# A hybrid streaming layer on one core: the order of its input projections

## The chip, the cores and the metric

One core of a Trainium2 chip runs the whole layer. The metric is the device time of one execution in microseconds, as the median of several runs. Engines are called TensorE (PE in the rows; PEld is its weight load), VectorE (DVE), ScalarE (ACT), POOL (GpSimd) and SP, which issues most DMAs.

## What is computed

One step of a streaming encoder for 1024 prompt frames and 32 sample frames, 1056 rows in all, model width 1024:

```python
xn = rms_norm(x, norm_mix)
zq, zk, zv, ziq, zik, ziw, zs = _split(xn @ w_in, (512, 256, 256, 512, 64, 8, 1696))
q  = rope_partial(rms_norm(zq, q_gain), pos)          # 8 heads of 64
k  = rope_partial(rms_norm(zk, k_gain), pos)          # 4 heads of 64
qi = rope_partial(ziq, pos); ki = rope_partial(layer_norm(zik), pos)   # indexer
score = sum_h relu(qi_h . ki / 8) * ziw_h / sqrt(8)   # over the keys a chunk may see
keep the top min(256, L // 4) keys of each query      # 256 for the prompt, 136 for the sample
o_att  = softmax(q . k / 8 over the kept keys) @ v
o_rwkv = rwkv7_time_mix(zs)       # token shift, decay, delta rule, group norm, gate; 8 heads
h = x + concat(o_att, o_rwkv) @ w_out
y = h + square(relu(rms_norm(h) @ w_ff1)) @ w_ff2     # hidden width 4096
```

Outputs are y, the keys, the values, the indexer keys, the RWKV state and the last row of zs.

## The kernel before

Every product in 32-bit numbers is made of three in a shorter format: both factors are split into a high and a low part (hi, lo), and high by high, high by low and low by high are added in PSUM. The normalised input stands transposed in SBUF as xh and xl for the whole of the projections. The weights are split where they are needed, in `wprep`: a DMA into `wraw` (three buffers), a ScalarE cast into `wh`, a POOL subtraction into `wl`. There are eight buffers of each in the set x and eight in the set y, exactly one weight group each.

Python code issues work in a chosen order, generators step several strands in turn, and a planner with a timeline of its own then fixes each engine's queue before the run; an engine takes its queue strictly in order. `high_priority(n)` moves instructions n ranks ahead in the planner's list. Memory is a stack of pools: a tile of a pool that was opened where another pool was closed waits for the readers of the tiles that lay there.

The order of the projections before:

- `main`: rows are normalised and transposed (`x_tile`), the indexer's keys and the values are projected (`key_tile`), then the indexer's queries, whose scores go to the tile G (`idx_tile`).
- `main2`: keys (9 tiles of 256 columns, W in set x), then queries (9 tiles of 512 columns, W in set y). Both use `norm_tile`: `proj_tok` (24 matmuls, 16 in the tile of the sample), a copy to the tile zq (three buffers), squares, sums, a power on POOL (`rsqrt_small`, L125), a VectorE multiply (L420), a gain multiply on POOL (L421), four rotation instructions on POOL (L221 to L224) and a DMA out. Queries go to `qd` in DRAM.
- `main3`: the RWKV inputs zs in 14 blocks (`zs_block`, list `ZB`; index 0 is the 64 columns of decay and learning rate, 1 the 96 of the gate, the others 128 columns of r, k or v). A block is 3 times 24 matmuls of 352 columns (L440), two ScalarE passes that empty each bank with the token shift (L449, L450), an addition on POOL (L452) and a DMA to `zsd` in DRAM. They run in seven groups; the third set z was opened for one of them in place of y.

The top-k of the indexer is two chains (`topk`): one with counts on VectorE (L342) for the row tiles 2, 3, 4 and 8, and one with sign passes on ScalarE (L362) for 5, 6 and 7. Each takes 32 steps, a bit of the threshold in each, and then makes the masks (L382 to L404). `step(n)` issues up to n steps of both chains after a tile or block.

The RWKV work is five units of up to 256 tokens. `rwkv_front` prepares a unit: step 1 loads k and makes norms and the decay's small products, step 2 sums the decay (L647), step 3 makes kk, exponentials, and the products k and tha (L669, L671), step 4 makes KB (L681) and the bonus; then come AR and the products G of its four chunks (L712, L715), and a triangular inverse on POOL (`lane_inverse`, L824 to L835). `rwkv_back` carries the state. Three rounds of unit 0's front are issued beside the last blocks (`EARLYF`). Step 4 needs the pool `rb`, which opens after the projections' pools are closed; attention's pool `at` follows it. Unit 1's KB and G are the top-k's tiles KB and G. Attention (`attn_all`, L1064 to L1146) and RWKV are then issued in turn; the output projection and the MLP (L1256, L1320, L1340) come last.

Of the kernel before, what the change touches and what calls it, by code (L numbers as in the profile page):

```python
# [55 lines left out]
BF16 = mybir.dt.bfloat16  # L56
I32 = mybir.dt.int32
AF = mybir.ActivationFunctionType
ALU = mybir.AluOpType
# [4 lines left out]
BIG = 3.0e38  # L64

T = 1056
NT = 9
# [7 lines left out]
def rows_of(t):  # L75
    return 128 if t < 8 else 32
# [74 lines left out]
def phase_a(S, pwx, pwy, pa, pi, px, xp, ps, late):  # L151
    nc, I, O = S.nc, S.I, S.O
# [7 lines left out]
    def wprep(tag, o, n, dve=True):  # L160

        W = []
        pool, size = {"x": (pwx, 328), "y": (pwy, 512), "z": (late.get("pz"), 128)}[tag]
        for k in range(8):
            raw = pwx.tile([128, 512], F32, name="wraw", bufs=3)
            c = 0
            for a, m in runs(o if isinstance(o, list) else [(o, n)]):
                nc.sync.dma_start(raw[:, c:c + m], w_in[k * 128:(k + 1) * 128, a:a + m])
                c += m
            hi = pool.tile([128, size], F32R, name="wh" + tag, bufs=8)  # L170
            lo = pool.tile([128, size], F32R, name="wl" + tag, bufs=8)
            (nc.vector.tensor_copy if dve and k % HIM < HID else nc.scalar.copy)(hi[:, :n], raw[:, :n])
            nc.gpsimd.tensor_tensor(lo[:, :n], raw[:, :n], hi[:, :n].bitcast(F32), op=ALU.subtract)
            W.append((hi, lo))
        return W

# [53 lines left out]
    for t in range(4, NT):  # L230
        n = 664 if t == 8 else 128 * (t + 1)
# [175 lines left out]
    def norm_tile(t, W, H, gain, dst):  # L407

        r = rows_of(t)
        n = H * 64  # L410
        z = pa.tile([128, 512], F32, name="zq", bufs=ZQB)[:r, :n]
        proj_tok(z, t, W, n)
        qk = z.rearrange("p (h d) -> p h d", h=H)
        sq = pa.tile([128, 8, 64], F32, name="sq", bufs=1)[:r, :H]
        nc.scalar.square(sq, qk)
        st = pa.tile([128, 2, 8], F32, name="stq", bufs=2)[:r, :, :H]
        nc.vector.tensor_reduce(st[:, 0], sq, AX.X, ALU.add)
        nc.vector.tensor_scalar(st[:, 0], st[:, 0], 1.0 / 64, 1e-6, op0=ALU.mult, op1=ALU.add)
        rsqrt_small(S, st[:, 1], st[:, 0], H)
        nc.vector.tensor_tensor(qk, qk, st[:, 1][:, :, None].to_broadcast([r, H, 64]), op=ALU.mult)  # L420
        nc.gpsimd.tensor_tensor(qk, qk, gains[:r, gain][:, None, :].to_broadcast([r, H, 64]), op=ALU.mult)  # L421
        rope(qk, t, H)
        nc.sync.dma_start(dst, z)
# [33 lines left out]
    def main():  # L457
        pend = [x_load(0)]
        nc.sync.dma_start(gbc, I["norms"][0:1].partition_broadcast(128))
        nc.sync.dma_start(S.ident, I["ident"])  # L460
        pend.append(x_load(1))
        nc.vector.memset(S.sc[8][:, 544:664], FMAX)
        for X in TK:
            nc.gpsimd.memset(X.cnt, 0.0)
            nc.gpsimd.memset(X.cns, 0.0)
            for j, t in enumerate(X.SL):
                n = S.sc[t].shape[1]
                for i in range(2):
                    nc.gpsimd.memset(X.off[:, i, j:j + 1], float(n - 256 - 256 * i))
        Wa = wprep("x", [(1536, 72), (768, 256)], 328, False)  # L470
        nc.sync.dma_start(cs, I["rope"][0])
        nc.sync.dma_start(sn, I["rope"][1])
        nc.sync.dma_start(gains, I["gains"].partition_broadcast(128))
        nc.sync.dma_start(S.pv, I["pvec"])
        for t in range(NT):
            if t + 2 < NT:
                pend.append(x_load(t + 2))
            x_tile(t, pend[t])
            if t >= LAG:
                key_tile(t - LAG, Wa)  # L480
            if t >= LAG + LAGT:
                key_turn(t - LAG - LAGT)
            if t == WBT:
                Wb = wprep("y", 1024, 512, False)
            if t == CKT:
                cache_keys()
            yield
        for t in range(NT - LAG, NT + LAGT):
            if t < NT:
                key_tile(t, Wa)  # L490
            key_turn(t - LAGT)
        late["W"] = wprep("x", 512, 256)
        for i, t in enumerate(IDXO):
            idx_tile(t, Wb)
            if i >= EI:
                for _ in range(EARLY):
                    next(tk[0], None)
            yield
# [3 lines left out]
    def step(n):  # L502
        for i, g in enumerate(tk):
            m = min(n, left[i])
            left[i] -= m
            for _ in range(m):
                next(g)

    mu1 = pwx.tile([128, 14], F32, name="mu1")

    def main2():
        nc.gpsimd.memset(S.shl, 0.0)
        nc.gpsimd.tensor_scalar(mu1, S.pv[:, 16:30], -1.0, 1.0, op0=ALU.mult, op1=ALU.add)
        W = late["W"]
        Wn = wprep("y", 0, 512)
        for t in range(NT):
            norm_tile(t, W, 4, 1, O["k_prompt"][t * 128:t * 128 + rows_of(t)] if t < 8 else O["k_sample"])
            step(STEP)
        late["W"] = wprep("x", *cols(0))
        for t in range(NT):  # L520
            norm_tile(t, Wn, 8, 0, S.qd[t * 128:t * 128 + rows_of(t)])
            if t == 8:
                S.mb[7] = S.mp.tile([128, 1024], BF16, name="mb7")
            step(STEP)


    gs = [("x", [0]), ("y", [2, 5, 8, 11]), ("x", [3, 6]), ("y", [9, 12]), ("x", [4, 7]), ("z", [10]), ("x", [13, 1])]

    def cols(j):
        o = [(1608 + ZB[i][0], ZB[i][1]) for i in gs[j][1]]  # L530
        return o, sum(n for _, n in o)

    def main3(pool, j0, j1):

        for j in range(j0, j1):
            W = late["W"]
            if j + 1 < len(gs):
                late["W"] = wprep(gs[j + 1][0], *cols(j + 1))
            c = 0
            for i in gs[j][1]:  # L540
                zs_block(i, W, c, pool, mu1)
                c += ZB[i][1]
                step(STEP)
                yield
        if j1 == len(gs):
            for t in range(2):
                n = 128 * (t + 1)
                nc.gpsimd.memset(S.mb[t], 0.0)
                nc.gpsimd.memset(S.mb[t][0:64, n - 64:n], -BIG)
            step(100)  # L550
            yield

    def masks():
        for g in tk:
# [803 lines left out]


STEP = 1  # L1360
PREI = 0
F0 = 200
F1 = 0
# [10 lines left out]
PTB = 2  # L1374
PRE = 2
EARLYF = 3
MA = 8
ATT0 = 0
BOFF = 300
# [5 lines left out]
RORD = (0, 1, 2, 3, 4)  # L1385
# [25 lines left out]
def body(tc, I, O, dbg=None):  # L1411
# [4 lines left out]
    with pool(name="const") as cp, pool(name="dram", space=DRAM) as dp:  # L1416
# [6 lines left out]
        def opened(name, side="left"):  # L1423
            p = pool(name=name, side=side)
            return p, p.__enter__()

        def close(*ps):
            for p in ps:
                p.__exit__(None, None, None)
# [5 lines left out]
        with pool(name="xnt") as xp, pool(name="psA", space=PSUM) as ps:  # L1435
            late = {}
            a_x, pwx = opened("pwx")
            a_y, pwy = opened("pwy")
            a_1, pa = opened("pa")
            with pool(name="pi", side="right") as pi:  # L1440
                with pool(name="px", side="right") as px:
                    m1, m2, m3, masks = phase_a(S, pwx, pwy, pa, pi, px, xp, ps, late)
                    g = m1()
                    for _ in range(NT):
                        next(g)
                with pool(name="pj", side="right") as late["pj"]:
                    for _ in g:
                        pass
            p1b, te = opened("p1b", "right")
            eq = te.tile([128, 2, 1024], F32, name="KB")  # L1450
            S.eq = [eq[:, i] for i in range(2)]
            with pool(name="pq", side="right") as pq:
                m2()
                close(a_1)
                for _ in m3(pq, 0, 4):
                    pass
            close(a_y)
            a_z, late["pz"] = opened("pz")
            rs, S.rs = opened("rs", "right")
            rf, S.rf = opened("rf", "right")  # L1460
            S.ps, S.pr = ps, ("pd", 6 - ACB)
            S.fronts = 0
            with pool(name="pq") as pq:
                g = m3(pq, 4, 7)
                next(g)
                rwkv_setup(S)
                S.kv = {(0, False): attn_load(S, 0, False)}
                gr = rwkv_all(S, RORD)
                for _ in range(EARLYF):
                    next(gr)  # L1470
                for _ in g:
                    pass
            close(a_z, a_x)
        rb, rp = opened("rb")
        at, S.at = opened("at")
        rf2, S.rf2 = opened("rf2", "right")
# [61 lines left out]
```

## Time and profile before

| what | us |
|---|---|
| median of 3 runs | 1797.38 (1795.8 to 1797.55) |
| the profiled execution | 1798.12 |
| its span, first to last instruction | 1796.3 |
| busy: TensorE / VectorE / ScalarE / POOL | 1663.9 / 936.1 / 707.6 / 618.6 |

The span is the time from the program's first instruction to its last; what lies around it is 1.8 us. A matmul is shown with its passage through the array, so that TensorE reads as busy when matmuls overlap; the spacing of their starts is what a stream of them costs. Instructions on POOL are rough. The granted clock of TensorE is 1.00 at 2.4 GHz and 0.50 at 1.2 GHz, and a stretch with both shows a mean.

### The profile page before, as it was taken

The numbers are of one execution on the slowest core, as the hardware profiler recorded it, in microseconds if no ns is written. First come the engines' busy times: TensorE is split into PE (matmuls) and PEld (weight loads), VectorE is DVE, ScalarE is ACT, GpSimd is POOL, SyncE is SP. The second block draws the span as 40 slices with busy tenths as digits, with TensorE's granted clock in tenths as the row PEclk, the third lists the DMA queues.
The fourth block names the chain that finished last, engine by engine and source line by source line (L and its number), as shares of the span: only waits on it lengthen the run. The fifth ranks groups of instructions, "written<-read, shape, count | busy, mean of one in ns | idle before, by whom it ended". The sixth has DMA issues, their size and how long they took to land.

```text
span 1796.3 us, 30013 instructions
## 1 busy us (share of the span) xinstructions
PE 1663.9 (93%) x11686; PEld 1509.2 (84%) x11686; DVE 936.1 (52%) x1996; ACT 707.6 (39%) x1549; POOL 618.6 (34%) x919
## 2 busy tenths in 40 slices
PE   7999979986569898999899999999999999999999
PEld 6787779986456777767678799999999999999998
DVE  6477889975878687577562533222222222222224
ACT  6365667897446344344641331222222121212120
POOL 7468863353543443056210021222222222222120
PEclk9999989996559697798899999999999999999999
DMA  7211131323110202140323341111111111111105
GB/s 218 54 36 43 42 88 64 110 68 92 29 27 14 40 24 57 26 101 17 98 76 123 121 125 49 46 48 45 49 37 53 42 53 42 47 44 51 36 16 172
DMA packets 180775, 113.25 MB, mean 63 GB/s; under 512 B 51969, under 2 KB 169817, under 8 KB 180633
## 3 DMA queue, kind: packets, MB, share of 16 engines
q1 hardware_dynamic: 171800, 107.00, 21.4%
q10 hardware_dynamic: 8832, 4.33, 0.9%
q8 instruction: 92, 1.51, 0.4%
q14 instruction: 51, 0.41, 0.1%
HBM read 86.29 MB, written 25.01 MB: 62 GB/s over the span
## 4 chain that ended last, share of the span: by engine, by line
PE 63%; DVE 12%; ACT 5%; POOL 4%; issue 3%; DMA 2%; SPq 0%; DVEq 0%; ACTq 0%; POOLq 0%
PE pd L1320 20%; PE pr L1340 10%; PE pc L1340 5%; PE po L1340 5%; PE pd L1256 3%; PE po L1139 2%; DVE AR L342 2%; ACT AR L362 2%; PE ptr L1123 2%; PE pr L1256 2%; PE acc L440 2%; DVE L L824 1%; PE pr L712 1%; POOL tl L829 1%; POOL Yl L831 1%
## 5 line engine op out<-in xcount | busy, mean ns | idle before, releaser
L1320 PE MATMUL pd<-hh,w1h 128*128 128x352 f32 x768 | 248.6, 324 | 2.2 <-issue 1.4
L1320 PE MATMUL pd<-hh,w1l 128*128 128x352 f32 x768 | 248.2, 323 | 0.7 <-DVE w1l L1187 0.7
L1320 PE MATMUL pd<-hl,w1h 128*128 128x352 f32 x768 | 247.5, 322 | 0.0
L1326 DVE TENSOR_TENSOR h2l<-rl,h2h 128x352 fp32r<-128x352 f32 x96 | 56.9, 592 | 277.3 <-ACT h2h L1325 277.3
L1324 POOL TENSOR_TENSOR rl<-rl 128x352 f32<-128x352 f32 x96 | 85.2, 888 | 215.5 <-ACT rl L1323 215.5
L1186 ACT CAST w2h<-w2r 128x512 fp32r<-128x512 f32 x64 | 39.7, 621 | 293.0 <-PE po L1340 144.8
L1320 PEld LDWEIGHTS pd<-hh,w1h 128*128 128x128 f32 x768 | 144.7, 188 | 2.8 <-issue 1.7
L1320 PEld LDWEIGHTS pd<-hh,w1l 128*128 128x128 f32 x768 | 144.8, 189 | 0.9 <-DVE w1l L1187 0.9
L1320 PEld LDWEIGHTS pd<-hl,w1h 128*128 128x128 f32 x768 | 145.3, 189 | 0.0
L1187 POOL TENSOR_TENSOR w2l<-w2r,w2h 128x512 fp32r<-128x512 f32 x32 | 41.6, 1299 | 299.3 <-ACT w2h L1186 288.8
L1340 PE MATMUL pr<-h2h,w2l 128*128 128x352 f32 x384 | 124.3, 324 | 0.0
L1340 PE MATMUL pr<-h2h,w2h 128*128 128x352 f32 x384 | 124.3, 324 | 0.0
L1340 PE MATMUL pr<-h2l,w2h 128*128 128x352 f32 x384 | 124.1, 323 | 0.0
L362 ACT ACTIVATE AR<-G,cnd 128x768 bf16<-128x768 f32 (+2 forms) x93 | 96.7, 1040 | 42.2 <-DVE cnd L367 36.8
L1323 ACT ACTIVATE rl<-pd 128x352 f32<-128x352 f32 x96 | 44.3, 463 | 143.4 <-PE pd L1320 136.9
L1346 DVE TENSOR_TENSOR ya<-ya,pr 128x352 f32<-128x352 f32 x84 | 43.8, 521 | 101.0 <-PE pr L1340 101.0
L829 POOL TENSOR_TENSOR tl<-L,Yl 128x56 f32<-128x56 f32 (+22 forms) x155 | 65.9, 425 | 60.5 <-DVE L L824 50.0
L1105 ACT ACTIVATE s<-s,m 32x544 f32<-32x544 f32 (+8 forms) x72 | 55.4, 770 | 74.8 <-DVE m L1102 74.6
L1123 PE MATMUL ptr<-ident,s 128*128 128x128 f32 (+2 forms) x328 | 69.4, 321 | 16.2 <-ACT s L1105 11.2
L1325 ACT CAST h2h<-rl 128x352 fp32r<-128x352 f32 x96 | 46.6, 485 | 75.3 <-POOL rl L1324 75.3
L1340 PEld LDWEIGHTS pr<-h2l,w2h 128*128 128x128 f32 x384 | 72.3, 188 | 0.1
L1340 PEld LDWEIGHTS pr<-h2h,w2h 128*128 128x128 f32 x384 | 72.2, 188 | 0.1
(443 smaller groups left out, 4655.1 us busy)
## 6 DMA issues: line engine op xcount, KB each, us to landing
w1r<-in_w_ff_dram SPq DMA_DIRECT2D x32, 512.0 KB, 4.1
w2r<-in_w_ff_dram SPq DMA_DIRECT2D x64, 256.0 KB, 2.9
zsd<-zm SPq DMA_DIRECT2D x12, 528.0 KB, 2.7
wraw<-in_w_in_dram SPq DMA_DIRECT2D x24, 256.0 KB, 2.7
wraw<-in_w_in_dram SPq DMA_DIRECT2D x40, 128.0 KB, 2.2
x<-in_x_prompt_dram SPq DMA_DIRECT2D x8, 512.0 KB, 5.0
hres<-hd ACTq DMA_DIRECT2D x16, 256.0 KB, 3.3
out_dram<-hres SPq DMA_DIRECT2D x16, 256.0 KB, 2.3
```

The costliest lines, as they stand in the source:

```text
L362: nc.scalar.activation(junk2[:r, :n], S.sc[t][:r, :n], AF.Sign, bias=c_of(j, r), scale=-1.0, accum_out=cnt[:r, j:j + 1])
L829: eng.tensor_tensor(t_, L[:, 0:j, j:j + 1].to_broadcast([128, j, w]), Y[:, j:j + 1, m:16].to_broadcast([128, j, w]), op=ALU.mult)
L1105: nc.scalar.activation(s, s, AF.Exp, bias=m[:, i:i + 1], scale=-1.0, accum_out=w.m[:, 6 + h:7 + h])
L1123: nc.tensor.transpose(p[:x, i, h, :r], w.s[h][:, c0 + i * 128:c0 + i * 128 + x], S.ident[:r, :r])
L1256: nc.tensor.matmul(acc[:r], a[:, k], b, start=(i == 0), stop=(i == 23))
L1320: nc.tensor.matmul(acc, a[:, k], m[:, k, o:o + n], start=(i == 0), stop=(i == 23))
L1323: nc.scalar.activation(rl, acc, AF.Relu)
L1324: nc.gpsimd.tensor_tensor(rl, rl, rl, op=ALU.mult)
L1325: nc.scalar.copy(h2h[:, o:o + n], rl)
L1326: nc.vector.tensor_tensor(h2l[:, o:o + n], rl, h2h[:, o:o + n].bitcast(F32), op=ALU.subtract)
L1340: nc.tensor.matmul(acc, a[:, k], m[:, o:o + n], start=(i == 0), stop=(i == 11))
L1346: nc.vector.tensor_tensor(y, y, acc, op=ALU.add)
```

## The change

The RWKV inputs come directly behind the indexer, in five groups that take the sets x and y in turn. Then set y is closed, the RWKV pools are opened, and the keys and the queries come last, the queries in two passes of 256 columns, all three with weights in set x. The three early rounds of unit 0's front are issued beside them, three tiles after each round (`KQ`), the rest of the tiles after that. A block issues two steps of the top-k (`ZSTEP`) in place of one, a tile one. The first load of attention's keys and values, and the masks of the first two row tiles, come after the last query tile. The pool `pa`, with the tiles of `norm_tile`, is opened below `pwy` and stays until the end of the projections.

```diff
-        pool, size = {"x": (pwx, 328), "y": (pwy, 512), "z": (late.get("pz"), 128)}[tag]
+        pool, size = {"x": (pwx, 328), "y": (pwy, 512)}[tag]
...
-        late["W"] = wprep("x", 512, 256)
+        late["W"] = wprep("x", *cols(0))
...
     def main2():
-        nc.gpsimd.memset(S.shl, 0.0)
-        nc.gpsimd.tensor_scalar(mu1, S.pv[:, 16:30], -1.0, 1.0, op0=ALU.mult, op1=ALU.add)
-        W = late["W"]
-        Wn = wprep("y", 0, 512)
-        for t in range(NT):
-            norm_tile(t, W, 4, 1, O["k_prompt"][t * 128:t * 128 + rows_of(t)] if t < 8 else O["k_sample"])
-            step(STEP)
-        late["W"] = wprep("x", *cols(0))
-        for t in range(NT):
-            norm_tile(t, Wn, 8, 0, S.qd[t * 128:t * 128 + rows_of(t)])
-            if t == 8:
-                S.mb[7] = S.mp.tile([128, 1024], BF16, name="mb7")
-            step(STEP)
-    gs = [("x", [0]), ("y", [2, 5, 8, 11]), ("x", [3, 6]), ("y", [9, 12]), ("x", [4, 7]), ("z", [10]), ("x", [13, 1])]
+        for c in (512, 0, 256):
+            W = late["W"]
+            if c < 256 or c == 512:
+                late["W"] = wprep("x", 0 if c == 512 else 256, 256)
+            for t in range(NT):
+                r = rows_of(t)
+                dst = S.qd[t * 128:t * 128 + r, c:c + 256] if c < 512 else O["k_prompt"][t * 128:t * 128 + r] if t < 8 else O["k_sample"]
+                norm_tile(t, W, 4, int(c == 512), dst)
+                step(STEP)
+                yield
+        S.mb[7] = S.mp.tile([128, 1024], BF16, name="mb7")
+        for t in range(2):
+            n = 128 * (t + 1)
+            nc.gpsimd.memset(S.mb[t], 0.0)
+            nc.gpsimd.memset(S.mb[t][0:64, n - 64:n], -BIG)
+        step(100)
+        yield
+    gs = [("x", [0, 3, 6]), ("y", [9, 12, 2, 5]), ("x", [8, 11]), ("y", [4, 7, 10, 13]), ("x", [1])]
...
-    def main3(pool, j0, j1):
-        for j in range(j0, j1):
+    def main3(pool):
+        nc.gpsimd.memset(S.shl, 0.0)
+        nc.gpsimd.tensor_scalar(mu1, S.pv[:, 16:30], -1.0, 1.0, op0=ALU.mult, op1=ALU.add)
+        for j in range(len(gs)):
             W = late["W"]
-            if j + 1 < len(gs):
-                late["W"] = wprep(gs[j + 1][0], *cols(j + 1))
+            late["W"] = wprep(gs[j + 1][0], *cols(j + 1)) if j + 1 < len(gs) else wprep("x", 512, 256)
             c = 0
             for i in gs[j][1]:
                 zs_block(i, W, c, pool, mu1)
                 c += ZB[i][1]
-                step(STEP)
-                yield
+                step(ZSTEP)
...
+ZSTEP = 2
+KQ = 3
...
             a_x, pwx = opened("pwx")
+            a_1, pa = opened("pa")
             a_y, pwy = opened("pwy")
-            a_1, pa = opened("pa")
...
             with pool(name="pq", side="right") as pq:
-                m2()
-                close(a_1)
-                for _ in m3(pq, 0, 4):
-                    pass
+                m3(pq)
             close(a_y)
-            a_z, late["pz"] = opened("pz")
...
-            with pool(name="pq") as pq:
-                g = m3(pq, 4, 7)
-                next(g)
-                rwkv_setup(S)
-                S.kv = {(0, False): attn_load(S, 0, False)}
-                gr = rwkv_all(S, RORD)
-                for _ in range(EARLYF):
-                    next(gr)
-                for _ in g:
-                    pass
-            close(a_z, a_x)
+            g = m2()
+            next(g)
+            rwkv_setup(S)
+            gr = rwkv_all(S, RORD)
+            for i in range(EARLYF):
+                next(gr)
+                for _ in range(KQ):
+                    next(g, None)
+            for _ in g:
+                pass
+            S.kv = {(0, False): attn_load(S, 0, False)}
+            close(a_1, a_x)
```

## Rows read from the trace of the kernel before

**Rows 1.** Windows by stage: stretch, length, busy us (instructions) by engine PE/PEld/DVE/ACT/POOL, clock, DMA.

```profile
114.00:219.00 105.00, 102.02 (x571) 85.34 (x569) 78.44 (x142) 60.34 (x140) 86.49 (x110) 1.00 0.15 44
219.00:252.00 33.00, 21.16 (x120) 18.25 (x120) 32.33 (x66) 20.63 (x42) 25.81 (x30) 0.90 0.33 85
252.00:416.00 164.00, 152.67 (x920) 149.64 (x920) 132.70 (x380) 134.76 (x296) 68.33 (x83) 0.97 0.25 78
416.00:514.00 98.00, 51.49 (x243) 41.16 (x241) 75.73 (x156) 49.68 (x108) 52.40 (x79) 0.53 0.23 51
514.00:617.00 103.00, 93.33 (x830) 74.49 (x830) 72.93 (x163) 50.31 (x117) 40.03 (x79) 0.73 0.14 28
```

**Rows 2.** Timeline at 416 us: start, length, engine, line, operation, count [idle before].

```profile
417.99 1.22 DVE L681 TENSOR_TENSOR KB<-k,D 64x1024 f32<-64x1024 f32 x1 [1.65 <-ACT zm L449]
418.04 5.50 POOL L681 TENSOR_TENSOR KB<-tha,D 64x1024 f32<-64x1024 f32 x2 [7.01 <-ACT zm L449]
```

**Rows 3.** Groups (busy, mean ns, idle before), 416 to 514 us; timeline of DVE behind.

```profile
L402 DVE TENSOR_TENSOR_SCAN KB<-ones,KB 128x768 f32<-128x768 f32 (+2 forms) x3 | 6.0, 2011 | 0.0
...
L403 DVE SCALAR_TENSOR_TENSOR KB<-KB,need,G 128x768 f32<-128x768 f32 (+2 forms) x3 | 3.9, 1284 | 0.0
...
L362 ACT ACTIVATE AR<-G,cnd 128x768 bf16<-128x768 f32 (+2 forms) x15 | 15.6, 1039 | 10.2 <-DVE cnd L367 10.0
...
504.88 1.44 DVE L403 SCALAR_TENSOR_TENSOR KB<-KB,need,G 128x1024 f32<-128x1024 f32 x1
...
516.35 1.22 DVE L681 TENSOR_TENSOR KB<-k,D 64x1024 f32<-64x1024 f32 x1
```

**Rows 4.** Timeline of PE: first and last of 20, 8 and 14 matmuls.

```profile
412.83 0.32 PE L440 MATMUL acc<-xl,whx 128*96 128x352 f32 x1
...
415.88 0.32 PE L440 MATMUL acc<-xh,wlx 128*96 128x352 f32 x1
...
125.72 0.28 PE L209 MATMUL acc<-whx,xl 128*128 128x256 f32 x1
...
126.55 0.28 PE L209 MATMUL acc<-whx,xh 128*128 128x256 f32 x1
...
199.96 0.39 PE L209 MATMUL acc<-wly,xh 128*128 128x512 f32 x1
...
202.97 0.39 PE L209 MATMUL acc<-why,xl 128*128 128x512 f32 x1
```

**Rows 5.** Groups by form on POOL, 114 to 175 us: a key tile's instructions.

```profile
L125 POOL TENSOR_TENSOR stq<-stq,mhalf 128x4 f32<-128x4 f32 x8 | 9.9, 1232 | 1.6 <-DVE stq L418 1.5
L421 POOL TENSOR_TENSOR zq<-zq,gains 128x256 f32<-128x256 f32 x8 | 9.2, 1148 | 4.0 <-issue 2.2 <-DVE zq L420 1.2 <-ACT rl L327 0.6
...
L221 POOL TENSOR_TENSOR rt<-zq,cs 128x64 f32<-128x64 f32 x8 | 5.2, 656 | 0.5
L224 POOL TENSOR_TENSOR zq<-rt,rt 128x64 f32<-128x64 f32 x8 | 4.4, 552 | 0.5
L223 POOL TENSOR_TENSOR rt<-zq,sn 128x32 f32<-128x32 f32 x8 | 2.5, 311 | 0.0
```

**Rows 6.** Timeline of POOL in the key stage.

```profile
141.90 1.38 POOL L421 TENSOR_TENSOR zq<-zq,gains 128x256 f32<-128x256 f32 x1 [0.60 <-DVE zq L420]
143.35 0.32 POOL L221 TENSOR_TENSOR rt<-zq,cs 128x64 f32<-128x64 f32 x1
...
147.38 0.73 POOL L421 TENSOR_TENSOR zq<-zq,gains 128x256 f32<-128x256 f32 x1 [0.59 <-issue]
...
149.73 1.00 POOL L125 TENSOR_TENSOR stq<-stq,mhalf 128x4 f32<-128x4 f32 x1
```

**Rows 7.** Groups by form on POOL, 252 to 416 us.

```profile
L173 POOL TENSOR_TENSOR wlx<-wraw,whx 128x256 fp32r<-128x256 f32 x14 | 10.0, 736 | 16.2 <-ACT whx L172 16.2
...
L671 POOL TENSOR_TENSOR tha<-tha,kk 128x1024 f32<-128x1024 f32 x1 | 3.7, 3653 | 0.0
L125 POOL TENSOR_TENSOR rn<-rn,mhalf 128x16 f32<-128x16 f32 x1 | 2.9, 2929 | 1.0 <-DVE cnd L365 1.0
```

More of the change, by code (lines that the diff above doesn't have):

```diff
@@ L542, in main3 @@
                 c += ZB[i][1]
-                step(STEP)
-                yield
[L545 to L551, printed above, removed]
+                step(ZSTEP)
     def masks():
```

## Prediction

> **What bounds the kernel now.** First the windows by stage [rows 1]. From 114 to 219 us TensorE has work nearly all the time (102.0 of 105 us), and again from 252 to 416 us (152.7 of 164). Then comes a hole: from 416 to 514 us it is busy 51.5 of 98 us, and at a granted clock of 0.53, the lower of the two levels nearly throughout. From 514 us on it is full again. So the kernel is TensorE's until 416 us and from 514 us, and the 98 us between belong to somebody else: VectorE, busiest there with 75.7 of 98 us, and POOL with 52.4.
>
> What starts at 416 us is read in the timeline [rows 2]. The last projection matmul issues at 415.9 [rows 4], and at 418.0 both VectorE (after 1.65 us) and POOL (after 7.01 us) begin KB, step 4 of the first RWKV front; its releaser is ScalarE's emptying of that last bank. KB is in the pool rb, which opens where the projections' tiles were. So steps 1 to 3 of front 0 can run beside projections, and step 4, attention and everything behind them cannot, in either order. I call this moment the handover; its time and the length of what follows decide the result.
>
> What fills the hole is read in the groups of VectorE and ScalarE from 416 to 514 us [rows 3]: scan and mask instructions of the top-k, 6.0 and 3.9 us in two of its groups on VectorE, and 15 sign passes of 1.04 us on ScalarE. The top-k's second chain is not done at the handover. Its last use of VectorE starts at 504.9 us, and KB of unit 1, which lies in the top-k's own tiles (KB and G), comes at 516.4 us.
>
> **The change, part by part.** Before 114 us nothing moves but which weights are split. The rest is three sums.
>
> *Projection order, first part.* The 14 RWKV blocks now follow the indexer. A block is 72 matmuls of 352 columns, whose starts are 0.161 us apart (19 steps in 3.05 us), so 1008 of them cost 162 us. Beside them remains the indexer's scoring, whose part of TensorE I get as a difference: 102.0 us in 114 to 219, less 208 key matmuls of 256 columns at 0.119 us (24.8) and 208 query matmuls of 512 columns at 0.232 us (48.3), leaves 29 [rows 1, 4]. TensorE idled 11.3 of 164 us in the old block stage; at that rate 191 us get 13 of stalls. 114 + 162 + 29 + 13 = 318 us for the end of the blocks. Splitting the queries costs TensorE nothing: twice 0.119 is 0.238 against 0.232. Doubling the top-k steps per block changes a rank in a list, no work; its price is ScalarE's queue, where the emptying of a bank may stand behind more sign passes; that is inside the 13.
>
> *Projection order, second part.* Now 27 tiles of 256 columns (9 key tiles, 18 half query tiles) come last: 624 matmuls of 0.119 us, 74 us of TensorE. But each also has six instructions on POOL. In the old key stage their means are 1.232, 1.148, 0.656, 0.552 and twice 0.311 us, 4.21 us a tile (the two quarter rotations counted alike) [rows 5]. Some are much shorter at times: in the timeline the gain multiply took 1.38 us and then 0.73, a power 1.00, a half rotation 0.32 [rows 6]. With these a tile costs 2.99 us. Between the power and the multiply POOL sat idle 0.59 to 0.60 us, for VectorE's multiply. So POOL needs 81 to 114 us, without gaps, where TensorE needs 74: POOL paces this stage. I take 3.4 us, somewhat below the middle, as scoring, whose VectorE work ran beside the old key tiles, is over by then: 92 us for 27. Added are 24 weight splits of 0.736 us (17.7) and front 0's power, tha product and k product, the last counted like tha (2.93 and twice 3.65; 10.2) [rows 7]. The gaps are 16 us, and I let these other pieces fill half: 8. Sum 128, so POOL is through at 446 us. Up to three tiles wait in the z buffers, so TensorE's last matmul is some 9 us (two to three tiles) earlier, and the handover falls at about 437 in place of 418: **19 us later**. Attention's pool lies partly over the tiles that POOL still works in, so it waits nearly until 446.
>
> The x weights now follow each other three times in the same eight buffers (last block to keys, keys to queries, half to half), where x and y took turns before. So a set can be split only as the one before is released. A set costs at least eight splits, 5.9 us on POOL, and three raw buffers make the later loads wait for splits; I price a turn at 7 us of TensorE. While POOL is behind, these lie under its backlog and cost nothing more; without that cover they are 21 us.
>
> *Moved pieces.* On SP's queue the 18 half-query writes take the place of 9, and the first key and value loads of attention come after them; the last block's write to DRAM no longer stands at the handover. The memsets of two masks and the clearing of the shift tile are a handful of short fills and off every path; setup and front steps 1 to 3, which ran beside the last five blocks, run beside keys and queries.
>
> *After the handover.* The top-k now has 19 us more before the handover, and no norm work beside its first steps. If it ends ahead of the handover, the hole loses 10 us and more of VectorE work and 15.6 us of sign passes [rows 3], and unit 1's KB need not wait until 516. The gain is at least nothing (if RWKV and attention share TensorE as tightly from the start as from 514 on, where it is busy 93.3 of 103 us to 617 [rows 1]); it is at most 46 us, as POOL's own work in the hole is 52.4 of its 98 us. I take **38**, near the upper end: unit 1's KB stands 98 us behind unit 0's and comes close behind the top-k's last instruction [rows 2, 3], so that this wait lies on the RWKV chain and not beside it.
>
> Sum: 19 - 38 = -19 us. The profiled execution took 1798.1 us (span 1796.3, the 1.8 us around it untouched), 0.04% over the median of the runs shown. That gives 1779, and against the median hardly less.
>
> One rule speaks against this. In rows, the same gain multiply takes 1.38 and 0.73 us [rows 6]. The Trainium skill (SBUF — State Buffer, "Who interferes with whom") says that GpSimd shares a port pair with VectorE under an exclusive lock, and that a VectorE instruction with two SBUF inputs shuts out a GpSimd instruction that reads. By it the moved tiles, now beside the front's two-input products, pay the long durations: 27 times 4.21 in place of 3.4, 22 us more, and the sum would be 1801, no gain. The rows agree that something doubles these durations, but not what.
>
> **The rivals.**
> *TensorE paces the keys and queries.* If POOL's pieces come near their shortest and the gaps are filled, the stage is 74 + 21 = 95 us and the handover is at 413, 5 earlier than before; with 46 after it, 1798 - 51 = 1747. For it: POOL is idle over half of the old block stage. Against it: it was already 86.5 of 105 us busy where these tiles ran. Chance 0.18.
> *POOL at contended durations, the other side.* Tiles of 4.21 plus the 0.60 us gap, 130, and 28 of other pieces make 158 us; the handover is at 467, 49 later. If then the hole shrinks only by the 25.5 us of those top-k groups, 1798 + 24 = 1822. It decides from a stage of about 147 us, some 4.1 us a tile with pieces and half the gaps unchanged. For it are the key tiles' means; against it, that those ran beside scoring's two-input products, which are gone here. The Trainium skill's rule above (SBUF — State Buffer) points to this side. Chance 0.18.
> *The hole does not shrink.* The later handover is paid and RWKV and attention take as long as before, because their chains, not the top-k, set the pace: 1798 + 19 = 1817. For it: TensorE's full stretch from 514 on. Chance 0.09.
> *The clock.* TensorE now has work for half the time in the key and query stage. It kept 0.90 with 21.2 of 33 us busy (219 to 252), but 0.53 with 51.5 of 98 [rows 1]. At the lower level 624 matmuls are 149 us, with turns 170: handover 70 later, 1798 + 70 - 38 = 1830. The Trainium skill (TensorE: Matmul & The Clock Gate, "Why this matters for your kernels") warns that idle gaps between bursts drop the clock to half. The first of the two rows does not agree, the second does. Chance 0.04.
> *The two cancel*, so that the order changes and the time does not: 0.09.
>
> **How the numbers follow.** The forecast, faster by 4 to 40 us, has 0.42. Faster by over 0.2% (about 3.6 us, what a measurement of this kernel can tell) is that and the first rival, 0.60; within it 0.09; slower the other three, 0.31. The range of 1743 to 1818 takes in the first rival's time and the third's and leaves out the clock and the far ends; the forecast's own range is 1758 to 1794.
>
> **What would show it.** Right: the last block matmul near 318 us; from there POOL nearly full with some 4 us a tile and TensorE with gaps; KB of unit 0 at about 437; the top-k's last mask before that; unit 1's KB less than 60 us behind unit 0's (now 98); handover to phase C's full TensorE some 38 us shorter. Wrong: sign passes after the handover, blocks that end past 335 because ScalarE's queue holds up the banks, or a stage of keys and queries beyond 147 us.

## The result, and the profile after

The changed kernel takes 1812.9 us (median of 6 runs, 1806.5 to 1819.1) against 1797.0 beside it (6 runs, 1795.8 to 1798.0): ratio 1.0089, 95% interval 1.0060 to 1.0118, 0.9% slower, where 1779, about 1% faster, was forecast; the time lies inside the stated range of 1743 to 1818, but on the other side of the kernel before. Its profiled execution took 1808.2 us with a span of 1806.4, 10.1 over the span before. That is the sum to be explained.

Windows of the changed kernel by stage (columns as in [rows 1]):

```profile
114.00:126.00 12.00, 12.00 (x78) 10.28 (x77) 5.72 (x7) 7.52 (x18) 10.09 (x9) 1.00 0.38 103
126.00:171.00 45.00, 30.41 (x132) 18.30 (x130) 42.77 (x65) 31.50 (x71) 0.13 (x2) 0.99 0.00 1
171.00:337.00 166.00, 158.78 (x959) 154.73 (x960) 144.69 (x428) 134.91 (x290) 54.51 (x64) 0.98 0.19 63
337.00:378.00 41.00, 35.33 (x239) 32.94 (x238) 19.12 (x55) 36.56 (x78) 28.62 (x43) 0.88 0.35 96
378.00:390.00 12.00, 0.74 (x7) 0.48 (x5) 9.69 (x21) 7.32 (x17) 12.00 (x20) 0.66 0.17 45
390.00:432.00 42.00, 34.28 (x209) 32.76 (x209) 29.50 (x58) 16.81 (x39) 33.67 (x53) 0.77 0.17 49
432.00:469.00 37.00, 29.17 (x208) 26.97 (x207) 12.34 (x30) 9.14 (x24) 31.13 (x67) 0.91 0.17 51
469.00:520.00 51.00, 31.82 (x149) 26.86 (x149) 41.64 (x76) 18.75 (x39) 24.24 (x31) 0.52 0.33 75
520.00:577.00 57.00, 43.70 (x339) 35.41 (x339) 46.17 (x96) 25.79 (x66) 36.03 (x74) 0.74 0.19 37
...
941.00:1806.00 865.00, 857.09 (x5204) 832.57 (x5202) 257.27 (x433) 186.70 (x341) 169.26 (x153) 1.00 0.22 64
```

The second line is the surprise. From 126 to 171 us TensorE is busy 30.4 of 45 us, POOL 0.13, DMA nothing: scoring runs alone, on VectorE (42.8). The blocks, which were to run beside it, fill TensorE only from 171 to 337. Then come keys and queries, 132 us with a stretch of 12 in which TensorE does next to nothing, and the handover at 469.

What held the blocks: first the changed kernel's waits, 114 to 171 us (engine, its line and tile, releaser: us in total, times, longest), then timelines of its ScalarE, TensorE and VectorE (as in [rows 2]):

```profile
POOL tm L431 <- DVE G L331: 46.2, 1, 46.2
```

```profile
170.30 0.55 ACT L449 ACTIVATE zm<-acc,mu 64x352 f32<-64x352 f32 x1 [1.64 <-DVE G L331]
...
171.34 0.56 PE L440 MATMUL acc<-xh,whx 128*64 128x352 f32 x1 [4.67 <-ACT tm L450]
...
468.71 1.22 DVE L678 TENSOR_TENSOR KB<-k,D 64x1024 f32<-64x1024 f32 x1
...
469.02 1.05 ACT L404 ACTIVATE mb<-KB 128x1024 bf16<-128x1024 f32 x1
...
519.95 1.19 DVE L678 TENSOR_TENSOR KB<-k,D 64x1024 f32<-64x1024 f32 x1
```

POOL waits 46.2 us to clear the first column of the first block's tile tm, and the first evacuation of a block (the copy of a full accumulator out of PSUM) starts at 170.3, as VectorE's last scoring instruction ends. Between 114 and 126 TensorE had filled both accumulators of block 0 and could go no further. The last lines answer to [rows 2, 3]: KB of unit 0 at 468.7 (before 418.0), the last mask at 469.0, KB of unit 1 at 520.0 (before 516.4), now 51 behind unit 0's instead of 98. The sign passes had ended at 386. The last phase starts at 941 (before 933). So: handover 51 later, the way from it to the last phase 43 shorter (472 against 515), the last phase 2 longer, sum 10.

### The profile page after: what moved, and what is told of

Its sections match the earlier page's. It is cut to its first block, busy times and chain, and to the rows that moved or that the text cites. A ratio compares the mean times of both kernels' runs of the same rounds, so it can differ in the third digit from the quotient of the medians.

```text
span 1806.4 us, 30591 instructions
## 1 busy us (share of the span) xinstructions
PE 1655.1 (92%) x11894; PEld 1507.4 (83%) x11894; DVE 933.0 (52%) x2024; ACT 714.0 (40%) x1559; POOL 610.5 (34%) x965
## 4 chain that ended last, share of the span: by engine, by line
PE 69%; DVE 13%; POOL 6%; ACT 5%; issue 4%; DMA 3%; SPq 0%; DVEq 0%; ACTq 0%; POOLq 0%
PE pd L1317 20%; PE pr L1337 10%; PE pc L1337 5%; PE po L1337 5%; PE acc L209 3%; PE pd L1253 3%; PE acc L440 3%; ACT AR L362 2%; PE ptr L1120 2%; DVE AR L342 2%; PE po L1136 2%; PE pr L1253 2%; PE pr L709 2%; DVE L L821 2%; DVE G L331 2%
## 5 line engine op out<-in xcount | busy, mean ns | idle before, releaser
L362 ACT ACTIVATE AR<-G,cnd 128x768 bf16<-128x768 f32 (+2 forms) x93 | 96.9, 1042 | 26.9 <-DVE cnd L367 24.2
L209 PE MATMUL acc<-whx,xh 128*128 128x256 f32 (+1 forms) x256 | 82.4, 326 | 24.3 <-ACT zq L212 21.0
L209 PE MATMUL acc<-wlx,xh 128*128 128x256 f32 (+1 forms) x256 | 83.6, 327 | 8.2 <-POOL wlx L173 7.9
L209 PE MATMUL acc<-whx,xl 128*128 128x256 f32 (+1 forms) x256 | 81.6, 319 | 0.0
L209 PEld LDWEIGHTS acc<-whx,xh 128*128 128x128 f32 x256 | 55.1, 217 | 28.3 <-ACT zq L212 23.6
```

The lines of the kernel that those rows point to most:

```text
L209: nc.tensor.matmul(acc[:r, :n], l, w[:, :n], start=(i == 0), stop=(i == 23))
L362: nc.scalar.activation(junk2[:r, :n], S.sc[t][:r, :n], AF.Sign, bias=c_of(j, r), scale=-1.0, accum_out=cnt[:r, j:j + 1])
```

## The experiments

The moments of each profile, in us (KB 0 and KB 1: first KB instruction of units 0 and 1; last mask: its end; last phase: first matmul of the output projection), and the median time, for e3, e5, e6, e7, e8 and e11 that of a single execution. The moments are those of the one profiled execution, which need not be the median one: in e1 it is the slowest of ten (1787.5 to 1807.3), in e14 the fastest of ten (1787.1 to 1804.8), in e15 the fastest of four (1770.1 to 1778.5):

| kernel | blocks end | KB 0 | last mask | KB 1 | last phase | time |
|---|---|---|---|---|---|---|
| before | 416 | 418 | 507 | 516 | 933 | 1797 |
| changed | 337 | 469 | 470 | 520 | 941 | 1812.9 |
| e1 room | 316 | 462 | 461 | 515 | 937 | 1798.1 |
| e2 keys | 361 | 457 | 459 | 509 | 939 | 1808.8 |
| e3 late top-k | 336 | 473 | 474 | 526 | 953 | 1821.8 |
| e4 before, top-k steps | 416 | 418 | 507 | 516 | 927 | 1795.9 |
| e5 shared buffers | 338 | 461 | 462 | 512 | 946 | 1815.8 |
| e6 gains on VectorE | 337 | 458 | 459 | 511 | 947 | 1816.0 |
| e7 before, top-k cut | 415 | 419 | 438 | 474 | 903 | 1769.6 |
| e8 top-k cut | 337 | 464 | 465 | 518 | 944 | 1816.3 |
| e10 e2+e5+e6 | 362 | 433 | 468 | 493 | 913 | 1786.7 |
| e11 no weight turns | 337 | 460 | 461 | 511 | 944 | 1811.6 |
| e12 e10+raw buffers | 355 | 424 | 459 | 482 | 913 | 1781.3 |
| e13 e1+e5+e6+raw | 313 | 422 | 462 | 482 | 911 | 1777.0 |
| e14 e5+e6+raw | 339 | 454 | 456 | 506 | 918 | 1799.9 |
| e15 before, e6+raw | 406 | 408 | 507 | 509 | 906 | 1777.6 |
| e16 before, e6 | 417 | 418 | 515 | 516 | 916 | 1786.9 |
| e17 before, raw | 412 | 414 | 513 | 514 | 918 | 1782.8 |

**Room for the first blocks (e1).** The masks' tiles become one, in which the first four blocks' zm and tm lie before the masks are made; a small tile elsewhere (jk) gets one buffer in place of two.

```diff
...
-        zm = pool.tile([128, T], F32, name="zm", bufs=ZMB)[:m]
-        tm = pool.tile([128, T], F32, name="tm", bufs=ZMB)[:m]
+        if i in MBI:                       # MBI = (0, 3, 6, 9)
+            zm, tm = S.mz[:m, 0:T], S.mz[:m, T:2 * T]   # where the masks come later
+        else:
+            zm = pool.tile([128, T], F32, name="zm", bufs=ZMB)[:m]
+            tm = pool.tile([128, T], F32, name="tm", bufs=ZMB)[:m]
...
```

> The changed kernel, but the first four blocks (0, 3, 6, 9) are evacuated into space that is free during scoring (the masks' tiles, which nothing writes before 326 us). Theory, the loss lies in space: after 125.8 us no block matmul ran until 171.3 because the two evacuation tiles of a block lie over the scoring's tiles. Then block matmuls run between 126 and 171 us, scoring ends later than 166 (about 185), the blocks end at about 320 instead of 337, keys and queries hand over at about 452 instead of 469, and the time is about 1790 (15 to 20 less than the changed kernel). Rival, the order in TensorE's or ScalarE's queue holds the blocks back whatever their space: still no block matmul between 126 and 171, blocks' end at 337, time 1806 to 1813.

Ratio 0.9998 to the kernel before (0.9978 to 1.0018). Windows of this kernel:

```profile
126.00:171.00 45.00, 45.00 (x278) 40.84 (x277) 29.61 (x43) 28.84 (x75) 12.02 (x13) 1.00 0.12 34
...
198.00:316.00 118.00, 111.57 (x674) 110.85 (x675) 106.59 (x322) 93.05 (x196) 38.82 (x47) 0.97 0.18 60
316.00:462.00 146.00, 101.80 (x656) 94.51 (x655) 103.34 (x269) 98.20 (x215) 111.58 (x178) 0.81 0.19 56
```

TensorE is busy 45.0 of the 45 us that were 30.4, and the blocks end at 316. Space it was. TensorE's scoring now ends at 198 instead of 167, top-k's second chain runs on to 420 (386 in the changed kernel) beside the keys and queries, and these take 146 us instead of 132: of 21 us won ahead, 7 are left at the handover. That the longer chain is what slows them is not shown: in e13 below it runs to 417 and the stage takes 109.

**The keys back beside scoring (e2).** Their tiles have space of their own. The sets of the block groups change places with it, and the blocks start with 9, 12, 2, 5.

```diff
...
-        for c in (512, 0, 256):
+        for c in cs_:          # (512,) ahead of the blocks, (0, 256) behind them
...
```

> The changed kernel, but the keys' projection stands where it stood before, right behind scoring in the order (its tiles have space of their own), then the blocks, then the two halves of the queries beside the preparation. Theory, TensorE's free time beside scoring is what the change lost: the keys take TensorE's idle time of the scoring (about 15 of 45 us between 126 and 171, and the slow clock there), GpSimd is idle there, and the stage behind the blocks loses the keys' 41 us and the 12 us turn from keys to queries (337 to 390). Handover at about 435 instead of 469, top-k still over before it, time about 1775. Rival, what is gained ahead is given back behind because top-k ends later and the stretch from handover to the last phase grows from 472 back to 515: time 1800 to 1815.

Ratio 1.0071 (1.0048 to 1.0093): the rival's time, but not for its reason. The handover gained 12 instead of 34, as the 18 query tiles alone took 96 us (361 to 457; 79 in the changed kernel, 390 to 469), and the way from it to the last phase was 482.

**Top-k's steps moved (e3, e4).** `STEP = 0, ZSTEP = 1` in the changed kernel, two steps a block in the kernel before.

> The changed kernel with top-k's steps issued late: one step with each block, none with a tile of keys or queries, the rest after the queries. Theory, the stretch from handover to the last phase shrank from 515 to 472 us because top-k was over before the handover: now top-k ends after the handover (about 500 or later) and the stretch grows back to 500 to 515, time 1830 to 1850. Rival, it shrank because the preparation of the first heads had been set up by then, whatever top-k does: the stretch stays within 5 us of 472 and the time within 10 of 1806, or under it, since VectorE and ScalarE have less to do beside the queries.

> The kernel before with one edit: two steps of top-k with each block instead of one, its order of projections kept. Theory, the order in the queues sets when top-k ends (one step per 8.0 us there, 6.9 in the changed kernel): ScalarE's chain ends at about 420 instead of 458, the masks at about 465 instead of 507, the wait behind the handover shrinks by 20 to 40, time 1757 to 1777. Rival, the chain is bound by its own engines beside the evacuations of the blocks, not by the order: end at 450 to 460, time 1795 to 1800.

Neither tested its theory. In e3 the planner pulled the steps forward all the same (sign passes end at 395, 386 in the changed kernel), and its one execution came out in neither range. In e4 the order of instructions on VectorE, ScalarE and POOL is that of the kernel before, so it measures what one program varies by: ratio 0.9999 (0.9990 to 1.0009), last phase at 927 in its profile, 933 in that of before.

**Top-k cut short (e7, e8).** The same edit in both kernels.

```diff
...
         for i in range(30, -1, -1):
+            if i < 11 and not X.exact:
+                yield
+                continue
...
```

> The kernel before, with the last 11 of the 31 steps of the second top-k chain left out, so that this top-k stops at a coarser threshold. Theory, unit 1's KB comes at the later of two times, 9 us behind the last mask (507 us) and 52 us behind unit 0's KB (418), and the rest of the run follows it: the masks now end at about 420, KB of unit 1 at about 470 instead of 516, the last phase starts at about 890 instead of 933, time about 1752. Rival, the stretch behind the handover is set by TensorE's work and clock, not by top-k: KB of unit 1 moves and the last phase still starts at 925 or later, time 1788 to 1798.

> The changed kernel with the same cut of the second top-k chain. Theory, top-k is over too early there already to set anything (masks at 470 at the latest, KB of unit 1 at 520 is 52 behind unit 0's at 469): what is left to gain is only ScalarE's and VectorE's time beside the keys and queries, under 10 us: time 1796 to 1810. Rival, top-k's steps beside the keys and queries are what slows that stage: its 132 us shrink by 20 or more, time under 1790.

Timelines of POOL and VectorE for e7, then its window from unit 1's KB on:

```profile
418.61 3.48 POOL L684 TENSOR_TENSOR KB<-tha,D 64x1024 f32<-64x1024 f32 x1 [9.33 <-ACT zm L452]
...
474.04 1.19 DVE L684 TENSOR_TENSOR KB<-k,D 64x1024 f32<-64x1024 f32 x1
```

```profile
474.00:903.00 429.00, 383.61 (x4241) 302.16 (x4242) 300.15 (x717) 205.81 (x510) 177.82 (x382) 0.83 0.20 49
```

The same handover, top-k's last mask at 438 instead of 507, and unit 1's KB comes 42 us sooner; 30 of them reach the last phase, and the one execution takes 27 us less. The changed kernel gets nothing from the same cut. So the old hole was top-k's, and the changed order had already closed it. Whether unit 1's KB waited for top-k's tiles or for its work on VectorE is not separated: the cut takes away both.

**One link of the key and query stage at a time (e5, e6, e11), then together (e14).**

```diff
...
-        z = pa.tile([128, 512], F32, name="zq", bufs=ZQB)[:r, :n]
+        if t % 2 == 0:                                             # e5
+            late["z"] = pa.tile([128, 512], F32, name="zq", bufs=ZQB)
+        z = late["z"][:r, t % 2 * 256:t % 2 * 256 + n]
...
-        nc.gpsimd.tensor_tensor(qk, qk, gains[...], op=ALU.mult)
+        nc.vector.tensor_tensor(qk, qk, gains[...], op=ALU.mult)   # e6
...
-            if c < 256 or c == 512:                                # e11
-                late["W"] = wprep("x", 0 if c == 512 else 256, 256)
...
```

> The changed kernel, but two neighbouring tiles of keys or queries share one 512-column buffer, so that twice as many 256-column tiles can be under way in the same space. Theory, the stage of keys and queries (337 to 469, 132 us) is held by its buffers: TensorE waits for accumulators (23.6 us) that ScalarE empties into tiles whose DMA is not through (22.3 us): the stage shrinks to about 110, the handover comes at about 447, and unit 1's KB 52 us behind it at about 500 (520 now); time about 1786. Rival, GpSimd's pace of 3.4 us a tile holds it (27 tiles and 17.6 us of weights make 110 of 132) and the buffers only pass its delay on: the stage stays over 125, time 1800 to 1812.

> The changed kernel with the multiplication by the gains (0.774 us a tile, 27 tiles) on VectorE instead of GpSimd. Theory, GpSimd paces the keys and queries: the stage (132 us) shrinks by about 21 to 111, handover at about 448, time about 1786. Rival, the chain of latencies and buffers paces them: the stage shrinks by under 7 us, time 1800 to 1812.

> The changed kernel, but no weights are loaded for the queries: both halves are computed with the keys' weights, which leaves out 16 of the 24 weight pieces of that stage (12 us on GpSimd, 6 on ScalarE, and their DMAs) and both turns. Theory, the turn from keys to queries stands open on TensorE (378.7 to 389.9) because the weights' pieces stand in ScalarE's and GpSimd's queues among the tiles' work: the stage shrinks from 132 to about 110 and no gap over 8 us is left on TensorE between its tiles. Rival, the preparation of the first head in GpSimd's queue (2.4, 2.9 and 2.9 us beside the key tiles) holds that stretch: the gap stays, and the stage shrinks by under 8.

The stage shrank from 132 to 123, 121 and 123 us: each theory had a part and none the whole. Without weight turns TensorE still stood open at 378 to 385, 400 to 409 and 423 to 426, and its evacuations waited 26.9 us for tiles whose DMA was not through (waits, 337 to 460 us):

```profile
ACT zq L212 <- DMA qd<-zq: 26.9, 6, 6.0
```

None of the three, one execution each, leaves the changed kernel's spread in time.

> The changed kernel, its first blocks still without room beside scoring (blocks' end at 337), with shared buffers, gains on VectorE and shared raw buffers together. Theory, keys and queries are held by several links at once (buffers, GpSimd, the weights' raw pieces), of which each eased alone gave 8, 11 and 9 of 132 us: together they give at least their sum, 28, handover at 441 or earlier, KB of unit 1 at 495 to 500, time 1778 to 1798. Rival, each edit frees the same slack, and it is the longer top-k beside them or the order of the two kernels with other orders that let the sum come out there: the stage stays at 118 to 124, handover at 457 or later, time 1800 to 1815.

Ratio 1.0010 (0.9990 to 1.0031), 13 us under the changed kernel. The stage took 115, in between. The sum of 28 had taken e11's part for that of the raw buffers, which were not tried alone in this order; but e5 and e6 alone make 20, and all three edits gave 17. So here the links overlap. With room for the first blocks they do not: there the same three edits take the stage from 146 (e1) to 109 (e13 below), 37 us. At the handover room alone is worth 7 us, the three edits alone 15, and both together 47.

**Everything together (e10, e12, e13).** The raw edit lets two weight pieces of 256 columns share a buffer:

```diff
...
+                if k % 2 == 0:
+                    late["r"] = pwx.tile([128, 512], F32, name="wraw", bufs=3)
+                raw = late["r"][:, k % 2 * 256:k % 2 * 256 + 256]
...
```

> Keys beside scoring (as in the run with the keys moved back, handover at 457 us), and for the queries both the shared buffers and the gains on VectorE. Theory, buffers and GpSimd's pace are links of one chain, so that the edits give 8 and 11 us alone and add up: the queries take 70 us instead of 88, handover at about 438, KB of unit 1 52 behind at about 490, and with 417 to 436 from there to the last phase and 865 behind it the time is 1774 to 1793, under the kernel before. Rival, a third link (the turns of the weights) holds the stage when both are eased: handover not before 448, time 1790 to 1805.

> The same, and two raw weight pieces of 256 columns share one buffer of 512, so that the DMA of the next set runs up to six pieces ahead instead of three. Theory, ScalarE's queue waits for raw weights (12.9 us beside keys and queries in the changed kernel) and holds the evacuations behind that wait: another 5 to 8 us off the queries, handover at about 431, time 1767 to 1786. Rival, the raw pieces come late because the weights' own tiles come free late, not for want of buffers: same as without, within 3 us.

> The changed kernel with all the remedies that keep its order: room for the first blocks' evacuation (blocks end at 316), shared buffers, gains on VectorE, shared raw buffers. Theory, keys and queries take about 110 us instead of the 142 of the run with room alone: handover at about 428, KB of unit 1 at the later of 480 and 9 behind the last mask (420 and some 45 us), so about 480, time 1764 to 1783. Rival, top-k's second chain, which runs beside the keys and queries up to 420 then, and the preparation hold the stage: handover not before 445, time 1785 to 1800.

All three beat the kernel before: 0.9949 (0.9934 to 0.9965), 0.9932 (0.9911 to 0.9953) and 0.9894 (0.9866 to 0.9923). Windows of e13:

```profile
126.00:171.00 45.00, 45.00 (x277) 40.94 (x277) 30.34 (x42) 29.06 (x75) 12.82 (x14) 1.00 0.12 34
171.00:313.00 142.00, 136.41 (x821) 133.70 (x819) 125.70 (x342) 109.68 (x228) 45.05 (x57) 0.99 0.20 66
313.00:422.00 109.00, 89.45 (x655) 85.40 (x653) 89.64 (x266) 88.10 (x202) 89.07 (x154) 0.91 0.25 72
```

Blocks' end 313 and 109 us to the handover, where the forecast had 318 and 119. The queries of e10 took 71 us, 25 less than those of e2. What the raw buffers add in e12 is not its theory's: of 9 us at the handover 7 lie ahead of the blocks' end, and the intervals of e10 and e12 overlap.

**The same edits in the old order (e15, e16, e17).**

> The kernel before, its order kept, with gains on VectorE and shared raw buffers for the keys. Theory, the order matters: keys and queries run beside scoring there and wait for nothing that these edits ease, and behind them top-k sets unit 1's KB (516): no gain, time 1790 to 1806. Rival, the edits are worth something in any order, and the best version's gain is theirs alone: time under 1785.

> The kernel before with the gains on VectorE alone. The two edits together took 10 us off the handover (418 to 408) and 20 off the stretch from unit 1's KB to the last phase (417 to 397), in which neither edit has an instruction. Theory, GpSimd's backlog behind the key and query tiles (their gains at 0.7 and 1.4 us) delayed the first blocks: the handover comes at about 409 with this edit alone. For the stretch behind it: if it depends on how the planner happens to order the work there, it comes out anywhere between 397 and 436, as in the runs so far; if the earlier handover brings it, it is 397 to 402 again and the time 1768 to 1780.

> The kernel before with the shared raw buffers for the keys' weights alone. Theory, GpSimd's backlog is what the pair of edits eased: the handover stays at 416 to 420 here. The stretch from unit 1's KB to the last phase has no instruction of this edit: if the planner's order sets it, it may come out anywhere between 397 and 436 and the time between 1775 and 1815; if the handover sets it, it stays at 417 and the time at 1797 within 4.

0.9884 (0.9859 to 0.9908), 0.9953 (0.9936 to 0.9969) and 0.9921 (0.9907 to 0.9936). So the best kernel's gain cannot be laid to the new order: two of its edits do as well without it. Nor did GpSimd's backlog explain it: with the gains alone the handover stayed at 418 and unit 1's KB at 516, and the run still gained, behind them; the raw buffers alone brought the handover to 414 and gained more. Windows from unit 1's KB to the last phase, of the kernel before and of e16:

```profile
516.00:933.00 417.00, 382.49 (x4148) 299.58 (x4146) 289.36 (x675) 196.42 (x486) 151.97 (x319) 0.83 0.20 47
```

```profile
516.00:916.00 400.00, 359.51 (x4091) 284.06 (x4091) 286.77 (x667) 194.48 (x478) 153.18 (x317) 0.85 0.20 48
```

No edit has an instruction there, but the planner wrote another order for it on every engine, and the clock is a little higher (0.85 against 0.83). This stretch is 411 and 417 in two profiles of the old program, 397 to 404 in e15 to e17, 429 in e7, and 412 to 436 in the changed order's kernels. What in the order sets it stays open.

## Why the prediction was wrong

**Projection order, first part: this step failed.** It let the blocks run beside scoring from 114 us and summed 114 + 162 + 29 + 13 = 318. The terms were good (with room, e1 and e13, 316 and 313), the "beside" was not: zm and tm of pool pq open where scoring's pools pj and pi were, just as KB opens over the projections' tiles. The old keys and queries had their tiles in pa, so they could run beside scoring, and the moved blocks could not. I had asked where KB lies and not where the tiles of the moved work lie. The sign I gave, blocks past 335, came (337), but not by ScalarE's queue as I wrote. Cost at the blocks' end: 19 us.

**Projection order, second part: a tile's cost on POOL right, POOL as the one pacer and 8 us of gaps wrong.** 3.4 us a tile was forecast; the groups by form on POOL, 337 to 469 us, read

```profile
L125 POOL TENSOR_TENSOR stq<-stq,mhalf 128x4 f32<-128x4 f32 x23 | 25.1, 1096 | 9.9 <-DVE stq L418 9.8
L173 POOL TENSOR_TENSOR wlx<-wraw,whx 128x256 fp32r<-128x256 f32 x24 | 17.6, 749 | 7.5 <-PE acc L440 6.4 <-ACT whx L172 1.1
L421 POOL TENSOR_TENSOR zq<-zq,gains 128x256 f32<-128x256 f32 x22 | 17.0, 774 | 9.6 <-issue 5.0 <-DVE stq L418 1.6 <-DVE cns L386 1.3
L224 POOL TENSOR_TENSOR zq<-rt,rt 128x64 f32<-128x64 f32 x22 | 8.7, 396 | 0.4
L221 POOL TENSOR_TENSOR rt<-zq,cs 128x64 f32<-128x64 f32 x22 | 8.5, 386 | 0.3
L222 POOL TENSOR_TENSOR rt<-zq,sn 128x32 f32<-128x32 f32 x22 | 8.4, 380 | 0.0
L223 POOL TENSOR_TENSOR rt<-zq,sn 128x32 f32<-128x32 f32 x22 | 7.1, 324 | 0.0
```

which is 3.36 a tile without the splits, and these 17.6 (17.7). But POOL was busy only 105.4 of the 132 us, idle for 27 where 8 of gaps had been counted, and taking the gains off it (e6, some 21 us of its work) shortened the stage by 11. Three waits of the same stretch show other links (columns as above):

```profile
PEld acc L209 <- ACT zq L212: 23.6, 11, 11.5
ACT zq L212 <- DMA qd<-zq: 22.3, 7, 6.0
...
ACT whx L172 <- DMA wraw<-in_w_in_dram: 12.9, 9, 2.4
```

TensorE waits for accumulators, and ScalarE, which empties them, for tiles whose DMA is not through and for raw weights: the engines hand each tile on in turn with three buffers between. So the turns of the weights and the gaps, which I let hide under POOL's backlog, stood open in part. The stage took 13 us more to the handover than forecast (132 against 119), and e5, e6, e11 and e14 show several links rather than one. The two misses do not simply add: with room for the blocks this one grows to 27 us (146 in e1), so that e1's handover at 462 is still 25 behind the forecast of 437. Why it grows stays open.

**After the handover: right.** 38 was taken from the hole, 43 came off (26 to 51 in its variants, 31 in e7), and e7 and e8 show the reason that was given, top-k. Better than a length: unit 1's KB comes 1 to 9 us behind the last mask when top-k is late (before, e15 to e17), and 51 to 60 behind unit 0's when it is not (the changed kernel and all its variants, e7). With the handover at 469 the second had become the bound, and 520 is not sooner than 516. What sets those 51 to 60 was not tried.

**The sum.** Handover 19 + 13 = 32 later than forecast, the way behind it 5 shorter, the last phase 2 longer: -19 + 32 - 5 + 2 = 10, the difference of the spans. The median is 5 above the profiled execution.

**The rivals.** The time lies nearest those of the two slower ones, without their mechanisms: the hole did shrink, and a tile took 3.36 us of POOL and not 4.21. The clock was 0.83 in the stage, not at the lower level. The gain multiply took 0.774 us in the new stage, against 1.148 among the old key tiles [rows 5]. The long durations had not gone but become rare: of its 22 full multiplies 21 took 0.72 to 0.74 us and one 1.70, beside a mask instruction of top-k. Rotations, which take 0.24 to 0.32 us at their shortest, show it too (timelines of POOL, then of VectorE):

```profile
405.02 1.76 POOL L221 TENSOR_TENSOR rt<-zq,cs 128x64 f32<-128x64 f32 x1
406.75 2.03 POOL L222 TENSOR_TENSOR rt<-zq,sn 128x32 f32<-128x32 f32 x1
...
404.78 1.88 DVE L402 TENSOR_TENSOR_SCAN KB<-ones,KB 128x768 f32<-128x768 f32 x1
...
406.72 2.01 DVE L402 TENSOR_TENSOR_SCAN KB<-ones,KB 128x896 f32<-128x896 f32 x1
```

Each ends some 0.1 us behind the two-input scan beside it. By the Trainium skill's rule on the shared port (SBUF — State Buffer, "Who interferes with whom") the long durations were to be feared beside the front's two-input products; these rows agree with the rule, but it bit mostly beside top-k's masks, and seldom. An estimate of what it cost here is 3.36 less the shortest 2.99 us, over 24 tiles: 9 us, where 22 were feared.

## What to carry to other kernels

When work is moved beside other work, look first where its output tiles lie and who read that space last: an engine with free time is no use while the tile to evacuate into belongs to the neighbour. In a wait with two bounds, work out both, since removing one gains only the way to the other. And where a planner writes the queues anew, run a control with the old order and the same small edits before a gain of 1% is laid to the order.

## What the runs showed of the hardware

The first stretch behind unit 1's KB has the same 339 TensorE instructions, in the same order, in the changed kernel (520 to 577 above) and in e5. First that window of e5, then the stretches that either kernel spent at the lower level, the changed kernel's ahead of e5's:

```profile
512.00:578.00 66.00, 55.01 (x339) 44.18 (x339) 46.27 (x96) 26.16 (x66) 35.97 (x74) 0.59 0.16 31
...
471.00:542.00 71.00, 48.26 (x231) 41.59 (x231) 55.01 (x118) 25.31 (x61) 41.99 (x67) 0.50 0.29 69
...
464.00:563.00 99.00, 77.41 (x361) 63.89 (x363) 69.43 (x141) 36.49 (x86) 54.36 (x96) 0.50 0.22 51
```

57 us at a granted clock of 0.74, 66 at 0.59. In both TensorE had been busy some 32 of 51 us before, at 0.52 to 0.53, and in one the clock rose at 542 us, in the other at 563. The 8 us that e5 gained at the handover were lost again here. The six runs of the changed kernel go the same way: 1806.5, 1808.2 and 1809.1 us at mean clocks of 0.939, 0.941 and 0.936, and 1816.7, 1818.3 and 1819.1 at 0.931, 0.929 and 0.931. The Trainium skill (TensorE: Matmul & The Clock Gate, "Why this matters for your kernels") warns of idle gaps between bursts; the row at 0.52, with TensorE idle 19 of 51 us, agrees. Why the clock rises sooner in one run was not found.
